# One core, two trunk branches: part of a modulation summed on VectorE, attention that rests at the end of gate sums, and position-bias transfers spread out

## The chip, the cores and the metric

One NeuronCore of a Trainium2 chip runs the whole program; seven other cores are idle. The metric is the time of one execution on the device, in microseconds (us), of which the median of several runs is taken. Smaller is better. All arithmetic is fp32: where TensorE multiplies, a number is split into a high part H and a low part L, and three products (H·H, L·H, H·L) stand for one.

## The reference, cut to what matters

One layer of a diffusion backbone is applied to 128 context tokens and 256 latent tokens, of width 2048. Each of the two token sets has its own condition vector.

```python
m = silu(cond) @ w_mod + b_mod            # 2048 x 12288: sh1, sc1, g1, sh2, sc2, g2
h = rms_norm(x, n1) * (1 + sc1) + sh1     # "norm 1"
q, k, v, u = split(h @ w_in)              # w_in 2048 x 4096
attn = neighbourhood or context attention, 16 heads of 64, with a position bias rpb
x = x + g1 * ((sigmoid(h @ w_gate) halves * (attn @ w_na, fft(u) @ w_fnet)) @ w_o)
h2 = rms_norm(x, n2) * (1 + sc2) + sh2
x = x + g2 * ((silu(g) * a) @ w_down),  a, g = split(h2 @ w_gate_up)
```

Norm 1's modulation needs sh1 and sc1, 2048 channels each, for both conditions. The channels are cut into 16 tiles of 128, called k-tiles here.

## The kernel before

The order of instructions on each engine is written out by hand, by Python generators. A **unit** is one load of weights, two k-tiles of 512 columns (one in places), as the tile `wraw`. `next_unit` is called before TensorE's products of each unit: ScalarE casts `wraw` into `wh`, VectorE subtracts into `wl` (both for a unit two ahead, `split_unit`), then work beside the products is ticked, and the next load is issued. `Paced` turns a generator into such work: at each tick `due` grows by `rate`, and once `due` is at least `least`, whole steps are run until less than one is left. The list `front` is ticked three times in a unit (twice in `next_unit`, once in `mid_unit`), the list `behind` once.

The input projection goes over k-tiles in four groups (`GROUPS`: 1, 2, 4 and 9 k-tiles), each of them over eight column chunks: 8, 8, 16 and 40 units. Products of a chunk gather in three PSUM buffers `mm` (of four), one for each 128 tokens; at the end of a chunk's group VectorE adds them to `acc` (L682).

`prep` (the generator `prepare`) makes norm 1's tokens beside that. For each entry of `MODS` (one k-tile, then five times three), `mod_sums` streams the columns of `w_mod` for sh1 and sc1 in (tile `wm`, four buffers) and lets TensorE multiply them with the condition vectors `csz`, into one PSUM tile (L404); ScalarE copies the sums out (`mrow`, L412), TensorE gathers them with a selector (L420, `sel`), three small VectorE operations make shift and scale, and `modulate` writes H and L of the k-tile's tokens. When `prep` ends, `rows` begins: it makes the other four modulations (sh2, sc2, g1, g2) on VectorE, a product and sum over `wmr` of 128 x 1024 at a time (`accr`, L327 and L329), and adds up over partitions with a matmul against ones (L338).

In the last group of the input projection `expand_rpb` copies the position bias in DRAM, seven transfers `s_rpb<-in_rpb` (L250), one in each unit. After it come the gates: eight blocks of eight units over `w_gate`, where `front` holds the Fourier branch and then attention (`br_work`) and `rows`. Each block fills all four `mm` buffers, and they are copied out in its last unit (`gst`, L1032), by ScalarE or, for the first two, by VectorE when attention has lately taken exponentials:

```python
(nc.vector.tensor_copy if f < 2 and any(soft) else nc.scalar.copy)(st, po[f][:, :TOK])
```

A pair of heads goes through attention in the ticks of the string `PAIR`: `s0 m0` are scores and maxima, `e0 i0` exponentials and inverses, `t0` the transposes, and so on. The rest of the program (projections, `w_o`, norm 2, SwiGLU) isn't touched.

Of the kernel before, what the change touches and what calls it, by code (L numbers as in the profile page):

```python
# [13 lines left out]
F32 = mybir.dt.float32  # L14
F32R = mybir.dt.float32r
AF = mybir.ActivationFunctionType
ALU = mybir.AluOpType
# [22 lines left out]
GROUPS = [(0, 1), (1, 2), (3, 4), (7, 9)]  # L40
ORDER = [6, 7, 0, 1, 2, 3, 4, 5]
DUE = [-1.4, 0, 0, 0]
PREP = [1.75, 1.8, 1.8, 1.8]
PAIR = "qk,b,pv,s0 m0,e0 i0,lq,s1 m1,e1 i1,,t0 lb,v,,t1,lv,"


# [55 lines left out]
def trunk_kernel(ctx: ExitStack, tc: tile.TileContext, io: dict):  # L102
# [163 lines left out]
    with ExitStack() as ph:  # L266
# [22 lines left out]


        ROWS = (2, 4, 3, 5)

        def row_weights():

# [77 lines left out]
        def depth_of(n):  # L372

            return 4 if n == 1 else 2

        def mod_weights(alloc):


            def load(kt0, n, k0):
                w, nk = n * P, depth_of(n)  # L380
                wm = alloc([P, 2, nk, w], "wm")
                for ty in range(2):
                    col = ty * D + kt0 * P
                    nc.sync.dma_start(
                        wm[:, ty],
                        w_mod[k0 * P : (k0 + nk) * P, col : col + w].rearrange("(k p) n -> p k n", p=P),
                    )
                return wm

            return Ahead(load, [(kt0, n, k0) for kt0, n in MODS for k0 in range(0, KT, depth_of(n))], 0)  # L390

        def mod_sums(src, kt0, n, alloc, out):

# [3 lines left out]
            for k0 in range(0, KT, nk):  # L397
                _, wm = src.take()
                for kk in range(0, nk, 2):
# [13 lines left out]
                        out.append(rows)  # L413
                    yield

        def mod_cols(kt0, n, rows):
# [12 lines left out]
            d = msc[0][:, kt0 : kt0 + n, :]  # L429
            nc.vector.tensor_add(d, m[:, :, 1], bc(bcol[:, KT + kt0 : KT + kt0 + n]))  # L430
            nc.vector.scalar_tensor_tensor(
                out=d, in0=d, scalar=1.0, in1=bc(ng[:, 0, kt0 : kt0 + n]), op0=ALU.add, op1=ALU.mult
            )
            yield


        with ExitStack() as pha:
            wmp = phm.enter_context(tc.tile_pool(name="wmp", bufs=4, side="right"))
            cpool = pha.enter_context(tc.tile_pool(name="cpool", bufs=12))
            tmp = pha.enter_context(tc.tile_pool(name="tmpa", bufs=2))  # L440

# [128 lines left out]
            def prepare():  # L570

                follow = columns_and_tokens(*MODS[0])
                while prepared[0] < 1:
                    yield next(follow)
                for k0, n in MODS[1:]:
                    for _ in mod_sums(src, k0, n, wme, sums):
                        next(follow, None)
                        yield
                    follow = columns_and_tokens(k0, n)
                    while k0 == 1 and prepared[0] < 3:  # L580
                        yield next(follow)
                for _ in follow:
                    yield

            prep = Paced(prepare())
            rows_psum["tile"] = md_tile

            def rows_and_columns():
# [63 lines left out]
            for gi, (k0, n) in enumerate(GROUPS):  # L652
                prep.due, prep.rate = DUE[gi], PREP[gi]
                prep.least = 3.6 if gi else 1
                if gi == len(GROUPS) - 1:
                    behind.append(Paced(expand_rpb()))
                    new_ring()
                for rate, ci in zip(CHUNKS, ORDER):
                    if gi == len(GROUPS) - 1:
# [153 lines left out]
                values()  # L813

        qks, vs, biases = [], [], []
        soft = deque(maxlen=3)

        def load_qk(hp):
# [27 lines left out]
        def attention_pair(hp, wk, values_before):  # L846
# [151 lines left out]
                    ("s", scores), ("m", maxima), ("e", exps), ("i", inverses), ("t", keys_first))},  # L998
            }
            for tick in PAIR.split(","):  # L1000
                for w in tick.split():
                    work[w]()
                soft.append("e" in tick)
                yield
# [13 lines left out]
        for fc8 in range(8):  # L1018
            po = [mm_tile() for _ in range(4)]
            sts = []  # L1020
            for u in range(0, KT, 2):
                wH, wL = next_unit()
                for f in range(4):
                    s = slice(f * P, (f + 1) * P)
                    if f == 2:
                        mid_unit()
                    for kk in range(2):
                        k = u + kk
                        mm3(po[f][:, :TOK], wH[:, kk, s], wL[:, kk, s], hH[k], hL[k], k == 0, k == KT - 1)
# [6 lines left out]
        br_work.drain()  # L1036
        front.clear()
        behind.append(rows)
        pha.close()
# [368 lines left out]
```

## Time and profile before

| | |
|---|---|
| median of 3 runs | 2051.44 us (2049.2 to 2052.01) |
| the profiled execution | 2052.19 us, of which the span of the trace 2050.4 |
| TensorE (PE) busy | 2025.8 us, 99% of the span |
| VectorE (DVE) busy | 1248.0 us, 61% |
| ScalarE (ACT) busy | 757.9 us, 37% |
| DMA read and written | 390.46 MB, mean 190 GB/s |

The profile is of one execution. A group row of it says how often an instruction of one line and shape ran, its busy time, its mean, and how long the engine had idled before it and for whom. A timeline row gives the start (from the span's begin), the duration, engine, line, what it writes and reads, and in brackets the idle time before it. Matmuls overlap in their pipeline, so a matmul's cost is read from the distance between starts and not from its duration. L404 means line 404 of the kernel before.

### The profile page before, as it was taken

The page shows a single profiled execution, that of the slowest core. Times are in us where ns is not written, and L with a number is a line of the kernel's source. Part 1 is how long each engine was busy: PE and PEld are TensorE (multiplying, and loading weights), DVE is VectorE, ACT ScalarE, POOL GpSimd, SP SyncE. Part 2 cuts the span into 40 slices and gives each one's busy share as a digit, 9 for nine tenths or more (in the row PEclk, how much of TensorE's full clock was granted, in tenths as well). Part 3 has the DMA queues.
Part 4 walks back from the last instruction along what each step waited for, and adds up shares of the span by engine and source line. Part 5 has one row for each costly group of instructions (what it writes and reads, how often), then busy time and mean ns, then how long its engine had stood idle before and what let it go on. Part 6 is the DMA issues. An engine that isn't in the chain of part 4 may idle for free.

```text
span 2050.4 us, 27528 instructions
## 1 busy us (share of the span) xinstructions
PE 2025.8 (99%) x10986; PEld 1843.8 (90%) x10986; DVE 1248.0 (61%) x1528; ACT 757.9 (37%) x1135; POOL 43.1 (2%) x92
## 2 busy tenths in 40 slices
PE   7999999999999999999999999999999999999999
PEld 4668788999999999889998999899989998999897
DVE  4746889788987777765854444545454334333456
ACT  4433232456665434334523332222222232223222
POOL 1000000000001000010000000000000000000000
PEclk9999999999999999999999999999999999999999
DMA  9996979677776776754455555455554444444453
GB/s 332 328 338 222 309 232 315 215 217 212 228 212 181 258 248 194 250 168 154 124 167 156 152 163 155 144 153 155 155 163 134 124 129 127 129 128 123 136 163 123
DMA packets 220384, 390.46 MB, mean 190 GB/s; under 512 B 28464, under 2 KB 77632, under 8 KB 220256
## 3 DMA queue, kind: packets, MB, share of 16 engines
q1 hardware_dynamic: 213088, 382.13, 59.5%
q10 hardware_dynamic: 4672, 6.31, 0.9%
q8 instruction: 86, 1.41, 0.3%
q0 software_dynamic: 2496, 0.27, 0.1%
q14 instruction: 42, 0.34, 0.1%
HBM read 371.81 MB, written 20.51 MB: 191 GB/s over the span
## 4 chain that ended last, share of the span: by engine, by line
PE 94%; DMA 3%; DVE 2%; ACT 1%; issue 0%; SPq 0%; ACTq 0%; DVEq 0%
PE mm L147 19%; PE mm L149 19%; PE mm L148 19%; PE at L147 11%; PE at L149 11%; PE at L148 11%; PE at L404 1%; DMA wm<-in_w_mod 1%; DMA wraw<-in_w_in 1%; PE at L893 1%; PE at L979 1%; PE at L958 1%; DMA wmr<-in_w_mod 1%; DVE accr L329 0%; DMA xc<-in_x_prompt 0%
## 5 line engine op out<-in xcount | busy, mean ns | idle before, releaser
L144 DVE TENSOR_TENSOR wl<-wraw,wh 128x1024 fp32r<-128x1024 f32 (+1 forms) x464 | 559.1, 1205 | 668.5 <-ACT wh L143 667.3
L143 ACT CAST wh<-wraw 128x1024 fp32r<-128x1024 f32 (+1 forms) x464 | 480.9, 1038 | 1032.0 <-PE at L148 272.9
L147 PE MATMUL mm<-hH,wh 128*128 128x384 f32 x1152 | 389.4, 338 | 2.4 <-DVE gst L1032 2.4
L149 PE MATMUL mm<-hH,wl 128*128 128x384 f32 x1152 | 385.5, 335 | 0.0
L148 PE MATMUL mm<-hL,wh 128*128 128x384 f32 x1152 | 385.2, 334 | 0.0
L329 DVE SCALAR_TENSOR_TENSOR accr<-wmr,csz,accr 128x1024 f32<-128x1024 f32 x240 | 304.8, 1278 | 5.2 <-DMA wmr<-in_w_mod 5.1
L147 PEld LDWEIGHTS mm<-hH,wh 128*128 128x128 f32 x1152 | 216.3, 188 | 8.1 <-issue 4.3
L148 PEld LDWEIGHTS mm<-hL,wh 128*128 128x128 f32 x1152 | 216.4, 188 | 0.0
L149 PEld LDWEIGHTS mm<-hH,wl 128*128 128x128 f32 x1152 | 216.2, 188 | 0.0
L147 PE MATMUL at<-hH,wh 128*128 128x384 f32 x640 | 213.9, 334 | 0.0
L149 PE MATMUL at<-hH,wl 128*128 128x384 f32 x640 | 213.9, 334 | 0.0
L148 PE MATMUL at<-hL,wh 128*128 128x384 f32 x640 | 213.8, 334 | 0.0
L147 PE MATMUL mm<-wh,hH 128*128 128x512 f32 x404 | 160.8, 398 | 1.9 <-ACT hH L548 1.2
L148 PE MATMUL mm<-wl,hH 128*128 128x512 f32 x404 | 158.1, 391 | 2.8 <-DVE wl L144 2.8
L149 PE MATMUL mm<-wh,hL 128*128 128x512 f32 x404 | 158.4, 392 | 0.7 <-DVE hL L144 0.4
L147 PE MATMUL mm<-wh,cH 128*128 128x512 f32 x352 | 137.1, 389 | 0.0
L149 PE MATMUL mm<-wh,cL 128*128 128x512 f32 x352 | 137.0, 389 | 0.0
L148 PE MATMUL mm<-wl,cH 128*128 128x512 f32 x352 | 137.0, 389 | 0.0
L147 PEld LDWEIGHTS at<-hH,wh 128*128 128x128 f32 x640 | 120.1, 188 | 1.0 <-ACT wh L143 0.8
L148 PEld LDWEIGHTS at<-hL,wh 128*128 128x128 f32 x640 | 120.1, 188 | 0.2
L149 PEld LDWEIGHTS at<-hH,wl 128*128 128x128 f32 x640 | 120.1, 188 | 0.0
L147 PEld LDWEIGHTS mm<-wh,hH 128*128 128x128 f32 x404 | 76.0, 188 | 25.6 <-issue 3.1
(283 smaller groups left out, 2633.5 us busy)
## 6 DMA issues: line engine op xcount, KB each, us to landing
wraw<-in_w_gate_up SPq DMA_DIRECT2D x176, 512.0 KB, 3.7
wmr<-in_w_mod SPq DMA_DIRECT2D x128, 512.0 KB, 4.9
wraw<-in_w_down SPq DMA_DIRECT2D x88, 512.0 KB, 3.7
wraw<-in_w_gate SPq DMA_DIRECT2D x64, 512.0 KB, 4.3
wm<-in_w_mod SPq DMA_DIRECT2D x80, 384.0 KB, 6.7
wraw<-in_w_in SPq DMA_DIRECT2D x56, 512.0 KB, 5.8
wraw<-in_w_o SPq DMA_DIRECT2D x32, 512.0 KB, 4.7
wraw<-in_w_fnet_proj SPq DMA_DIRECT2D x16, 512.0 KB, 4.9
```

What stands on the lines that cost most here:

```text
L143: nc.scalar.copy(H, x)
L144: nc.vector.tensor_sub(L, x, fr(H))
L147: nc.tensor.matmul(out, aH, bH, start=start, stop=False)
L148: nc.tensor.matmul(out, aH, bL, start=False, stop=False)
L149: nc.tensor.matmul(out, aL, bH, start=False, stop=stop)
L329: nc.vector.scalar_tensor_tensor(out=acc[:, cnd], in0=wm, scalar=sc, in1=acc[:, cnd], op0=ALU.mult, op1=ALU.add)
L404: nc.tensor.matmul(pm[q : q + 32, :w], csz[:, k, :], wm[:, ty, kk + par, :], start=k < 2, stop=k >= KT - 2, tile_position=(0, q), skip_gro ...
L893: nc.tensor.matmul(po[j][:, cols], qx[rows[j], q], kx[rows[j], k], start=i == 0, stop=i == 2, tile_position=(j * HD, 0),)
L958: nc.tensor.transpose(o[:, i * P : (i + 1) * P], sc[:, j, c0 : c0 + P], ident)
L979: nc.tensor.matmul(po[j][:, CTX:TOK].rearrange("p (t q) -> p t q", t=2), w[1 + kc], x.rearrange("p (t b) q -> p t b q", t=2)[:, :, 2 * kc ...
```

## The change

Three things are done.

1. The last entry of `MODS` (k-tiles 13 to 15) leaves `mod_sums`. A new generator `late_sums` loads its weights in 32 pieces `wd` of 128 x 384 (192 KB, five buffers; before: eight tiles `wm` in 16 transfers of 384 KB), and VectorE multiplies and sums them for both conditions into four accumulators `late`, which live in the buffers of tokens not yet made. It is ticked in `behind` from the second group on, 1.6 pieces in a unit. When all are summed, `late_rows` adds up over partitions with four matmuls against `hot` (a column of ones at the condition's place), ScalarE copies the sums out, and `mod_cols` goes on as before. `prep` goes at 1.6 instead of 1.8 steps in a unit in the third and fourth group.
2. In the last unit of each gate block, a tick of attention that takes exponentials waits three ticks, and `rows` runs only once three steps are due.
3. The seven `s_rpb` transfers go one in five units.

```diff
-PREP = [1.75, 1.8, 1.8, 1.8]
+PREP = [1.75, 1.8, 1.6, 1.6]
+LATE = 1.6
...
+        def late_sums(kt0, n):
...
+            got = Ahead(load, [(k, ty) for k in range(KT) for ty in range(2)], 5)
+            yield
+            for k in range(KT):
+                for ty in range(2):
+                    if k + ty:
+                        got.more()
+                    _, wd = got.take()
+                    for a, sc in zip(late_acc[ty], (csz[:, k, cnd : cnd + 1] for cnd in range(2))):
+                        if k == 0:
+                            nc.vector.tensor_scalar_mul(a, wd, sc)
+                        else:
+                            nc.vector.scalar_tensor_tensor(
+                                out=a, in0=wd, scalar=sc, in1=a, op0=ALU.mult, op1=ALU.add
+                            )
+                    yield
+        def late_rows(kt0, n, alloc, out):
...
+            for ty in range(2):
+                for cnd, a in enumerate(late_acc[ty]):
+                    q = 32 * (2 * ty + cnd)
+                    nc.tensor.matmul(
+                        pm[q : q + 32, :w], hot[:, cnd], a, start=True, stop=True,
...
+            rows = alloc([P, w], "mrow")
+            nc.scalar.copy(rows, pm[:, :w])
...
-                for k0, n in MODS[1:]:
+                for k0, n in MODS[1:-1]:
...
-                for _ in follow:
+                yield from follow
+                while late.live:
+                    late.step()
                     yield
+                late_rows(*MODS[-1], wme, sums)
+                yield
+                yield from columns_and_tokens(*MODS[-1])
...
+                if gi == 1:
+                    behind.append(late)
                 if gi == len(GROUPS) - 1:
-                    behind.append(Paced(expand_rpb()))
+                    behind.append(Paced(expand_rpb(), 0.2))
...
             for tick in PAIR.split(","):
+                for _ in range(3 if ending[0] and "e" in tick else 0):
+                    yield
...
+                ending[0] = u == KT - 2
+                rows.least = 3 if ending[0] else 1
                 wH, wL = next_unit()
```

On TensorE, the last sums of the modulation stood before as a block of `wm` products, and two units later the selector; here are the rows around the selector in the third group (`mm` gathers the projection, `at` another PSUM tile):

```order
L147 MATMUL mm_1487<-wh_1409,hH_205_972 128x512
L148 MATMUL mm_1487<-wl_1410,hH_205_972 128x512
L149 MATMUL mm_1487<-wh_1409,hL_206_973 128x512
L420 MATMUL at_1516<-sel,mrow_1460 128x4 x3
L147 MATMUL mm_1485<-wh_1433,hH_209_986 128x512
L148 MATMUL mm_1485<-wl_1434,hH_209_986 128x512
```

And in the change, one unit later in the program:

```order
L148 MATMUL mm_1559<-wh_1501,hH_231_1059 128x512
L149 MATMUL mm_1559<-wl_1502,hH_231_1059 128x512
L150 MATMUL mm_1559<-wh_1501,hL_232_1060 128x512
L459 MATMUL at_1626<-late_670,hot 32x384
L459 MATMUL at_1626<-late_671,hot 32x384
L459 MATMUL at_1626<-late_672,hot 32x384
L459 MATMUL at_1626<-late_673,hot 32x384
L471 MATMUL at_1633<-sel,mrow_1631 128x4 x3
L148 MATMUL mm_1619<-wh_1560,hH_162_723 128x512
```

The selector now follows the matmuls whose copied sums it reads at once. The 64 products of `wm` for the last entry are gone from the rows between; from the second group to this place the blocks of such small products between the units number eight, where they were ten.

On VectorE, in the second group of the input projection, two chunks followed each other like this (`wl` the low weights of a unit to come, `xT` the scaling of a token tile, `acc` the sums of a chunk):

```order
L144 TENSOR_TENSOR wl_750<-wraw_604,wh_749 128x1024
L527 TENSOR_TENSOR xT_267<-xT_267,rB_310 128x384
L682 TENSOR_TENSOR acc_455<-acc_455,mm_746 128x512
L682 TENSOR_TENSOR acc_455<-acc_455,mm_747 128x512
L682 TENSOR_TENSOR acc_455<-acc_455,mm_748 128x512
L144 TENSOR_TENSOR wl_781<-wraw_641,wh_780 128x1024
```

and in the change, at the chunk before that one and this one:

```order
L445 TENSOR_SCALAR late_670<-wd_674,csz 128x384
L445 TENSOR_SCALAR late_671<-wd_674,csz 128x384
L445 TENSOR_SCALAR late_672<-wd_676,csz 128x384
L445 TENSOR_SCALAR late_673<-wd_676,csz 128x384
L742 TENSOR_TENSOR acc_424<-acc_424,mm_707 128x512
L742 TENSOR_TENSOR acc_424<-acc_424,mm_708 128x512
L742 TENSOR_TENSOR acc_424<-acc_424,mm_709 128x512
L145 TENSOR_TENSOR wl_777<-wraw_611,wh_776 128x1024
L579 TENSOR_TENSOR xT_274<-xT_274,rB_317 128x384
L447 SCALAR_TENSOR_TENSOR late_670<-wd_678,csz,late_670 128x384
L447 SCALAR_TENSOR_TENSOR late_671<-wd_678,csz,late_671 128x384
L742 TENSOR_TENSOR acc_462<-acc_462,mm_773 128x512
```

Two or four operations on `late` stand in each unit ahead of the sums that empty PSUM.

On ScalarE, at the end of the fourth gate block, exponentials (`sc,sm<-sc,mx`) and their scaling stood ahead of the copies `gst`:

```order
L143 CAST wh_4599<-wraw_4347 128x1024
L932 ACTIVATE sc_4438,sm_4603<-sc_4438,mx_4597 128x384 x2
L942 ACTIVATE sc_4438<-sc_4438,sm_4603 128x384 x2
L1032 COPY gst_4636<-mm_4116 128x384
L1032 COPY gst_4644<-mm_4117 128x384
```

In the change they come behind the next unit's cast:

```order
L144 CAST wh_4683<-wraw_4434 128x1024
L1097 COPY gst_4711<-mm_4197 128x384
L1097 COPY gst_4719<-mm_4198 128x384
L1100 DMA s_gate_94<-gst_4695 128x384
L1100 DMA s_gate_94<-gst_4703 128x384
L1100 DMA s_gate_94<-gst_4711 128x384
L1100 DMA s_gate_94<-gst_4719 128x384
L144 CAST wh_4733<-wraw_4480 128x1024
L993 ACTIVATE sc_4506,sm_4737<-sc_4506,mx_4681 128x384 x2
L1003 ACTIVATE sc_4506<-sc_4506,sm_4737 128x384 x2
```

Attention's later steps move with them. There are two such rests in the program, and attention ends two units later than before, with two and a half units of gate products still behind it.

## Rows read from the trace of the kernel before

**Rows 1.** The page: the span, the engines' busy times, and the shares of the chain of work that ended last.

```profile
span 2050.4 us, 27528 instructions
PE 2025.8 (99%) x10986; PEld 1843.8 (90%) x10986; DVE 1248.0 (61%) x1528; ACT 757.9 (37%) x1135; POOL 43.1 (2%) x92
...
PE 94%; DMA 3%; DVE 2%; ACT 1%; issue 0%; SPq 0%; ACTq 0%; DVEq 0%
```

**Rows 2.** All waits of TensorE from 165 to 2040 us: who waited for whom, us in total, times, the longest.

```profile
PE mm L148 <- DVE wl L144: 2.8, 2, 2.0
PE mm L147 <- DVE gst L1032: 2.4, 2, 1.5
PE at L149 <- DVE uL L144: 0.8, 1, 0.8
```

**Rows 3.** The timeline of TensorE around the last block of `wm` products but for the selector.

```profile
149.59 0.39 PE L148 MATMUL mm<-wl,hH 128*128 128x512 f32 x1
149.81 0.39 PE L149 MATMUL mm<-wh,hL 128*128 128x512 f32 x1
150.13 2.79 PE L404 MATMUL at<-wm,csz 128*32 128x384 f32 x32
152.85 0.50 PE L147 MATMUL mm<-wh,hH 128*128 128x512 f32 x1
153.19 0.40 PE L148 MATMUL mm<-wl,hH 128*128 128x512 f32 x1
```

**Rows 4.** Groups by shape, whole run: the sums over partitions that `rows` makes on TensorE.

```profile
L338 PE MATMUL at<-accr,ones 128*32 128x512 f32 x64 | 9.1, 605 | 0.0
```

**Rows 5.** The timeline of TensorE at two selectors: one right behind the products whose sums it reads, one two units behind them.

```profile
46.06 1.25 PE L404 MATMUL at<-wm,csz 128*32 128x384 f32 x8
47.90 0.83 PE L420 MATMUL at<-sel,mrow 128*128 128x4 f32 x6 [0.58 <-ACT mrow L412]
...
161.14 0.73 PE L420 MATMUL at<-sel,mrow 128*128 128x4 f32 x6
```

**Rows 6.** Busy time of the engines in stretches: us, then PE, PEld, DVE, ACT and POOL busy, the granted clock, the DMA share, GB/s.

```profile
20.00:50.00 30.00, 26.65 (x153) 13.99 (x152) 13.96 (x27) 11.88 (x22) 0.00 (x0) 0.89 1.06 369
60.00:100.00 40.00, 39.92 (x245) 27.11 (x244) 27.23 (x42) 13.34 (x20) 0.00 (x0) 1.00 0.95 322
100.00:160.00 60.00, 60.00 (x354) 41.98 (x353) 29.09 (x42) 21.55 (x32) 0.00 (x0) 1.00 0.90 312
195.00:225.00 30.00, 30.00 (x134) 24.86 (x133) 23.60 (x22) 7.74 (x8) 0.00 (x0) 1.00 1.04 365
```

**Rows 7.** Groups by shape of VectorE, the first two from 60 to 100 us, the others of the whole run.

```profile
L144 DVE TENSOR_TENSOR wl<-wraw,wh 128x1024 fp32r<-128x1024 f32 x8 | 9.8, 1224 | 3.1 <-ACT wh L143 3.1
L527 DVE TENSOR_TENSOR xT<-xT,rB 128x384 f32<-128x384 f32 x5 | 2.8, 552 | 0.0
...
L329 DVE SCALAR_TENSOR_TENSOR accr<-wmr,csz,accr 128x1024 f32<-128x1024 f32 x240 | 304.8, 1278 | 5.2 <-DMA wmr<-in_w_mod 5.1
...
L327 DVE TENSOR_SCALAR accr<-wmr,csz 128x1024 f32<-128x1024 f32 x16 | 11.8, 746 | 0.0
```

**Rows 8.** First the timeline of SyncE, which issues the loads; then the chain of waits between 74 and 97 us (start, us, what); then DMA issues of the whole run with size and median time to landing.

```profile
72.28 4.57 SPq L384 DMA_DIRECT2D wm<-in_w_mod  x8
...
76.39 7.09 DMA wm<-in_w_mod
...
94.07 2.72 PE at L404 x32
...
wm<-in_w_mod SPq DMA_DIRECT2D x80, 384.0 KB, 6.7
...
wraw<-in_w_in SPq DMA_DIRECT2D x16, 256.0 KB, 6.5
```

**Rows 9.** Timelines around the longest wait of the middle of the run: SyncE's issues (two of the seven `s_rpb`), ScalarE's cast, VectorE, TensorE.

```profile
204.03 0.66 SPq L250 DMA_DIRECT2D s_rpb<-in_rpb  x1
...
208.09 0.55 SPq L250 DMA_DIRECT2D s_rpb<-in_rpb  x1
...
222.83 1.05 ACT L143 CAST wh<-wraw 128x1024 fp32r<-128x1024 f32 x1 [4.61 <-DMA wraw<-in_w_in]
...
224.12 2.48 DVE L329 SCALAR_TENSOR_TENSOR accr<-wmr,csz,accr 128x1024 f32<-128x1024 f32 x2 [3.89 <-DMA wmr<-in_w_mod]
...
228.31 1.22 DVE L144 TENSOR_TENSOR wl<-wraw,wh 128x1024 fp32r<-128x1024 f32 x1
...
229.58 0.50 PE L148 MATMUL mm<-wl,hH 128*128 128x512 f32 x1 [2.02 <-DVE wl L144]
```

**Rows 10.** Timelines at the ends of two gate blocks: ScalarE, VectorE and TensorE at 504 us, TensorE at 639 us.

```profile
503.87 1.12 ACT L942 ACTIVATE sc<-sc,sm 128x384 f32<-128x384 f32 x2 [0.23 <-DVE sm L940]
...
503.75 1.27 DVE L329 SCALAR_TENSOR_TENSOR accr<-wmr,csz,accr 128x1024 f32<-128x1024 f32 x1
504.94 1.02 DVE L1032 COPY gst<-mm 128x384 f32<-128x384 f32 x2
...
505.54 0.44 PE L147 MATMUL mm<-hH,wh 128*128 128x384 f32 x1 [1.48 <-DVE gst L1032]
...
639.42 0.44 PE L147 MATMUL mm<-hH,wh 128*128 128x384 f32 x1 [0.94 <-DVE gst L1032]
```

More of the change, by code (lines that the diff above doesn't have):

```diff
@@ L291, in trunk_kernel @@
         ROWS = (2, 4, 3, 5)
+        late_acc = []
+        hot = consts.tile([P, 2, 32], F32, tag="hot", name="hot")
+        nc.vector.memset(hot, 0.0)
+        for cnd in range(2):
+            nc.vector.memset(hot[:, cnd, cnd : cnd + 1], 1.0)
         def row_weights():
@@ L388, in load @@
                 return wm
-            return Ahead(load, [(kt0, n, k0) for kt0, n in MODS for k0 in range(0, KT, depth_of(n))], 0)
+            return Ahead(load, [(kt0, n, k0) for kt0, n in MODS[:-1] for k0 in range(0, KT, depth_of(n))], 0)
         def mod_sums(src, kt0, n, alloc, out):
@@ L414, in mod_sums, with load @@
                     yield
+        def late_sums(kt0, n):
+            w = n * P
+            def load(k, ty):
+                wd = wdp.tile([P, w], F32, tag="wd", name=nm("wd"))
+                c0 = ty * D + kt0 * P
+                nc.sync.dma_start(wd, w_mod[k * P : (k + 1) * P, c0 : c0 + w])
+                return wd
+            for ty in range(2):
+                late_acc.append(
+                    [hpool.tile([P, w], F32, tag=f"t{c}{KT - 3 + ty}", name=nm("late")) for c in "HL"]
+                )
[12 more added lines that the diff above has]
+                                out=a, in0=wd, scalar=sc, in1=a, op0=ALU.mult, op1=ALU.add
+                            )
+                    yield
+        def late_rows(kt0, n, alloc, out):
+            w = n * P
+            pm = at_tile()
+            for ty in range(2):
+                for cnd, a in enumerate(late_acc[ty]):
+                    q = 32 * (2 * ty + cnd)
+                    nc.tensor.matmul(
+                        pm[q : q + 32, :w], hot[:, cnd], a, start=True, stop=True,
+                        tile_position=(0, q), skip_group_check=True,
+                    )
+            rows = alloc([P, w], "mrow")
+            nc.scalar.copy(rows, pm[:, :w])
+            out.append(rows)
         def mod_cols(kt0, n, rows):
@@ L438, in trunk_kernel @@
             wmp = phm.enter_context(tc.tile_pool(name="wmp", bufs=4, side="right"))
+            wdp = phm.enter_context(tc.tile_pool(name="wdp", bufs=5, side="right"))
             cpool = pha.enter_context(tc.tile_pool(name="cpool", bufs=12))
@@ L581, in prepare @@
                         yield next(follow)
-                for _ in follow:
+                yield from follow
+                while late.live:
+                    late.step()
                     yield
+                late_rows(*MODS[-1], wme, sums)
+                yield
+                yield from columns_and_tokens(*MODS[-1])
             prep = Paced(prepare())
+            late = Paced(late_sums(*MODS[-1]), LATE)
             rows_psum["tile"] = md_tile
@@ L815, in trunk_kernel @@
         qks, vs, biases = [], [], []
+        ending = [False]
         soft = deque(maxlen=3)
@@ L1036, in trunk_kernel @@
         br_work.drain()
+        rows.least = 1
         front.clear()
```

## Prediction

> **What bounds the kernel now.** I read the page first: TensorE is busy for 2025.8 of 2050.4 us, and the chain of work that ended last lies on it for 94% [rows 1]. The reader is to see from this that time can be won only by taking work from TensorE or by closing its gaps. The list of its waits then says how much there is of the second kind: between 165 and 2040 us six waits, 2.8 us for low weights `wl`, 2.4 us for gate copies, 0.8 us for a Fourier operand [rows 2]. So no single edit can bring much there, and the work taken away has to be priced by the distance of starts. Last I read the stretch where work is added to other engines: from 60 to 100 us VectorE is busy for 27.2 of 40 us, from 100 to 160 for 29.1 of 60, and the DMA engines have shares of 0.95 and 0.90, where 1.06 with 369 GB/s is the most that a stretch shows [rows 6]. TensorE hardly waits there, yet both others have little left in the first 40 us. Whether they carry the new work is the question of this change.
>
> **The modulation's last entry.** 64 products of `wm` go. A block of 32 stands from 150.13 to 152.85 us, 2.72 us or 85 ns each [rows 3]; two such blocks are 5.4 us, all on TensorE's path. Entering a block costs 0.32 where a start otherwise follows after 0.22 to 0.23, leaving it 0.34 [rows 3], some 0.2 us for a block; the order shows two fewer, so another 0.4 us goes. Added are four matmuls against `hot`. In fp32 the trace shows two passes for one, so eight; by the rows of `rows`' sums, which are 512 wide, they cost at most 8 x 9.1 / 64 = 1.1 us [rows 4], by 85 ns each 0.7. I take 0.8. New too is a wait: the selector now comes right behind the matmuls whose sums ScalarE has first to copy. The nearest row has a gap of 0.58 us there, and the one that stands two units off has none [rows 5]. In the change a cast of 1.05 us [rows 9] is queued on ScalarE just ahead of that copy, so the bounds are 0.6 and 1.6; I take 0.9. Behind the waiting selector all of TensorE's queue stands still. Sum of this part: -5.4 - 0.4 + 0.8 + 0.9 = -4.1 us.
>
> **What VectorE gets for it.** 64 operations of 128 x 384, of which the trace has none. From above, the 1024-wide sum takes 1.28 us [rows 7]; that it were no faster at 384 bounds it. From below 0.28, the 1024-wide plain product (0.75) scaled by width. The nearest row by width is 0.55 (`xT`, two SBUF operands, 384), and I take that. About 22 fall between 60 and 100 us: 27.2 + 22 x 0.55 = 39.3 of 40 us, full to the brim; the other 42 find 29.1 + 23 of 60. What is queued behind a late operation on VectorE are the three `acc` sums, which free PSUM, and the next `wl`. Both have room: `wl` is made two units ahead (a unit is 18 products at 0.23, 4.1 us), and with four buffers for three tiles a unit's sums are wanted only well into the unit after. So I cost it at nothing; if the cover goes, each unit pays its excess.
>
> **What the DMA queue gets.** The bytes are the same, but come earlier: about 15 pieces of 192 KB, 2.9 MB, before 100 us, where those of the old entry all came later. 322 GB/s becomes 322 + 2.9 MB / 40 us = 395, above the 369 of the fullest stretch: 1.0 MB too much, 2.8 us. The cushion: the loads issued from 72.28 us on feed products at about 84 and at 94 us, their landing takes 6.7 us in the median, and the chain of waits has one of them landing at 83.5 [rows 8], where TensorE is about to want it. Of the 2.8 us I expect 0.5 to reach TensorE, between the bounds 0 and 2.8; later the groups stand a unit further apart, and 6.3 MB less is wanted. SyncE's queue also waits for the slot of a `wd` piece ahead of `wraw` and `wm`; the five buffers are about three units, so I cost that at nothing beyond it.
>
> *A rule against this.* The rows show 256 KB transfers landing after 6.5 us where 384 KB take 6.7 [rows 8], in a queue that is seldom empty [rows 6], so small pieces don't pay for themselves alone. The Trainium skill ("DMA: Bandwidth & Descriptors", section Bandwidth) wants transfers of 1 MiB or more, and gives 138 GB/s for 64 KB and 341 for 1 MB. By it the new pieces would move at perhaps two thirds of the rate (an estimate from that page); the trace doesn't show it at these sizes, and it is a rival below.
>
> **Gate ends.** At 505.54 and 639.42 us TensorE waits 1.48 and 0.94 us for VectorE's copies of the block's sums [rows 10]. At the first, scaling of exponentials (until 505) and an `accr` of 1.27 us stand ahead of the copies on ScalarE and VectorE. The change puts both behind the copies; the order shows it. Next late there is the copy itself, 0.5 us, under the products of the other tiles. I take -2.2 of the 2.4; bounds -2.4 and 0, the latter if other steps of attention now meet a block's end. The two units by which attention ends later are covered: two and a half units of products remain.
>
> **The bias transfers.** From 195 to 225 us the DMA share is 1.04 [rows 6], with transfers of `s_rpb` unit by unit. A `wraw` comes late, ScalarE's cast idles 4.61 us for it, a `wmr` stops VectorE for 3.89, and the `wl` behind them ends at 229.5, which costs TensorE 2.02 us [rows 9]. With one in five units this pile-up doesn't form: I take -2.0, bounds -2.0 and 0. The other wait for `wl` (0.8 us) and the Fourier one stay. `rows` starts about two units later and moves as a whole; its results are wanted far behind.
>
> Sum: -4.1 + 0.5 - 2.2 - 2.0 = -7.8 us. Against the profiled 2052.19 that is 2044.4; that execution lies 0.75 above the median of the runs, so the prediction for the median is 2043.6 us.
>
> **Rivals.**
> *The loads bound the stretch up to 100 us.* For it: the DMA share of 0.95 there; against it: transfers issued 10 us ahead. The whole 2.8 us shows instead of 0.5, and the selector waits 1.6 instead of 0.9: -4.8, or 2046.6.
> *Small transfers are slow (the rule).* If a 192 KB piece took the queue as long as a 384 KB one, 1.07 us at 369 GB/s instead of 0.53, 15 pieces would add 8 us to the 2.8. Less some 3 us of cushion, about 7.8 arrive: the gain is gone, 2051. Against it are the landing times [rows 8].
> *The two later gaps only move.* Attention and `rows` stand otherwise against the blocks, and a full queue can form at another place; four of the 4.2 us come back: 2047.6. For it: VectorE is busy 23.6 of 30 us there [rows 6].
> *VectorE becomes the bound, and the kernel slower.* Its place is the second group of the input projection, 60 to 100 us, where it decides from 0.55 us for an operation on: above that, 22 operations no longer fit into 40 us, the `acc` sums come late and PSUM stops TensorE. At the upper bound of 1.28 us it is 22 x 0.73 = 16 us: -8 + 16, or 2059.5. At 0.9 it would just eat the gain. Against it: two rows of 1024 and 384 give 1.05 ns a column, so 0.6 at most.
>
> **Chances.** Forecast 0.60 (own range 2041 to 2046.5), the loads 0.15, the rule 0.04, the gaps that move 0.13, VectorE 0.08. Less than 0.2%, 4.1 us, is about what a measurement of this kernel can't tell from no change: faster than that is below 2047.3. Nearly all of the forecast and of the loads, and a little under half of the gaps that move, are that: 0.58 + 0.13 + 0.05 = 0.76; the same for the rest and the rule, 0.16; VectorE is the slower side, 0.08. The range runs from 2040.5, where every bound falls well, a third wait of 0.8 us goes too and the runs lie as far down as the lowest of before (2.2 us under the median), to 2049.5, which takes in the loads and the gaps that move.
>
> **What will show it.** Group rows: the products of `wm` 256 instead of 320, the late sums at 0.5 to 0.6 us each. In the timeline of TensorE: no wait over 1 us between 60 and 165 us but for one of about 0.9 at the selector behind `late`. From 60 to 100 us VectorE at 38 to 40 of 40 us. In the list of waits after 165 us: `gst` gone or under 0.3 us, one `wl` of 0.8 left. TensorE's busy time down by about 4.5 us. I'm wrong if `wm` or `acc` ends waits of TensorE up to 165 us that add up to 3 us or more, if `gst` or `wl` stand in the list with 2 us at other places, or if the late sums take 0.8 us.

## The result: slower, and the profile after

The changed kernel takes 2059.82 us in the median of four runs (2058.91 to 2063.64), the kernel before beside it 2051.73; the ratio is 1.0046, with a 95% interval of 1.0034 to 1.0059. I had forecast 2043.6, faster, in a range up to 2049.5. The profiled execution took 2058.91 us. It is the fastest of the four, so that its trace explains 6.7 us (spans of 2057.1 and 2050.4) and not the whole 8.1 between the medians. In what follows "the changed kernel" is this one, and lines of its code are its own (L404 of before is L410, L338 is L344, L682 is L742, L1032 is L1097).

First the page of the changed kernel: the span, the engines, the chain that ended last.

```profile
span 2057.1 us, 27536 instructions
PE 2025.6 (98%) x10930; PEld 1846.1 (90%) x10930; DVE 1280.2 (62%) x1595; ACT 756.5 (37%) x1135; POOL 44.1 (2%) x92
...
PE 91%; DMA 3%; DVE 3%; ACT 1%; issue 1%; SPq 1%; ACTq 0%; DVEq 0%
```

Beside [rows 1] the reader sees that TensorE is as busy as ever (2025.8 before), though 64 products went, and that the span is 6.7 us longer. Busy time can only stay while work goes if what is left ran slower. Then all waits of TensorE from 60 to 2040 us (who for whom, us in total, times, the longest), which answer to [rows 2]:

```profile
PE mm L148 <- DVE gst L1097: 4.0, 2, 3.6
PE mm L148 <- DVE acc L742: 3.3, 1, 3.3
PE at L344 <- DVE accr L335: 2.1, 1, 2.1
PE at L150 <- DVE uL L145: 0.8, 1, 0.8
PE mm L149 <- DVE wl L145: 0.8, 1, 0.8
PE at L471 <- ACT mrow L418: 0.6, 1, 0.6
PE at L471 <- ACT mrow L464: 0.6, 1, 0.6
PE at L344 <- DVE pt L145: 0.5, 1, 0.5
PE at L410 <- DMA wm<-in_w_mod: 0.2, 1, 0.2
```

The wait of 2.0 us for `wl` has gone, as forecast. Three new ones stand there, each for VectorE: `acc`, `gst` and `accr`. Where the time went stage by stage is read from the start of the same weight split `wl` (the k-th of 464, counted from 0) in both traces:

| k-th `wl` | start before | after | difference | what lies between |
|---|---|---|---|---|
| 8 | 52.04 | 50.97 | -1.1 | start of the run; differs between executions by as much |
| 36 | 191.31 | 193.18 | +1.9 | modulation with late sums: +2.9 |
| 60 | 284.84 | 283.95 | -0.9 | bias transfers: -2.8, of which 2.0 are the wait |
| 88 | 405.99 | 404.98 | -1.0 | |
| 144 | 702.34 | 705.85 | +3.5 | gate blocks with attention: +4.5 |
| 172 | 823.39 | 830.02 | +6.6 | gates' products, where `rows` sums: +3.1 |

From there to the end the difference stays at 6.6. So four places make the result: the bias transfers, which gain, and three stops of TensorE, which are shown now.

**The stop for `acc` at 153 us.** Timelines of the changed kernel, VectorE first (start, us, engine, line, out<-in, how many in a row), then TensorE:

```profile
148.86 1.22 DVE L145 TENSOR_TENSOR wl<-wraw,wh 128x1024 fp32r<-128x1024 f32 x1 [0.74 <-ACT wh L144]
150.29 0.56 DVE L145 TENSOR_TENSOR hL<-hf,hH 128x384 fp32r<-128x384 f32 x1 [0.21 <-ACT hH L144]
151.72 0.56 DVE L145 TENSOR_TENSOR hL<-hf,hH 128x384 fp32r<-128x384 f32 x1 [0.87 <-ACT hH L144]
153.16 0.56 DVE L145 TENSOR_TENSOR hL<-hf,hH 128x384 fp32r<-128x384 f32 x1 [0.88 <-ACT hH L144]
153.63 2.20 DVE L447 SCALAR_TENSOR_TENSOR late<-wd,csz,late 128x384 f32<-128x384 f32 x4
155.75 1.88 DVE L742 TENSOR_TENSOR acc<-acc,mm 128x512 f32<-128x512 f32 x3
...
152.79 0.39 PE L150 MATMUL mm<-wh,hL 128*128 128x512 f32 x1
156.49 0.50 PE L148 MATMUL mm<-wh,hH 128*128 128x512 f32 x1 [3.31 <-DVE acc L742]
157.41 0.63 PE L148 MATMUL mm<-wh,hH 128*128 128x512 f32 x1
157.83 0.63 PE L149 MATMUL mm<-wl,hH 128*128 128x512 f32 x1
```

`prep` prepares three tokens in one unit here. Their three `hL` stand in VectorE's queue, and each waits for ScalarE, so that 1.7 us of work last from 150.3 to 153.7. Behind them come four late sums, 2.2 us, and only then the three `acc` sums, which empty the PSUM buffers that TensorE needs at 153.0. It stands for 3.31 us.

The same unit of the kernel before (its `wl` is the one with k = 27, as here) holds one token, and the `acc` sums wait for TensorE:

```profile
151.32 1.23 DVE L144 TENSOR_TENSOR wl<-wraw,wh 128x1024 fp32r<-128x1024 f32 x1 [2.84 <-ACT wh L143]
152.75 0.56 DVE L144 TENSOR_TENSOR hL<-hf,hH 128x384 fp32r<-128x384 f32 x1 [0.21 <-ACT hH L143]
154.54 0.69 DVE L682 TENSOR_TENSOR acc<-acc,mm 128x512 f32<-128x512 f32 x1 [1.23 <-PE mm L149]
```

So the change puts two more tokens into this unit, and not only the late sums. Before, three tokens stood in one unit too, at 95 us, right ahead of `acc` sums; there a block of 32 `wm` products stood on TensorE beside them (94.00 to 96.72 us), and no wait shows. The three tokens at 150 us in the changed kernel have no such block beside them. That this cover is what is missing wasn't tried by itself.

After the stop, TensorE's starts are 0.43 us apart instead of 0.23, and the windows show why (from:to, us, busy times of PE, PEld, DVE, ACT and POOL, the granted clock, the DMA share, GB/s):

```profile
153.00:156.00 3.00, 0.17 (x1) 0.00 (x0) 2.84 (x6) 1.07 (x2) 0.00 (x0) 1.00 0.07 10
157.00:158.00 1.00, 1.00 (x4) 0.77 (x4) 1.00 (x3) 0.00 (x0) 0.00 (x0) 0.56 0.99 373
158.00:160.00 2.00, 2.00 (x7) 1.54 (x6) 2.00 (x4) 0.00 (x0) 0.00 (x0) 0.50 0.32 56
161.00:162.00 1.00, 1.00 (x6) 0.84 (x5) 0.00 (x0) 0.87 (x1) 0.00 (x0) 1.00 0.77 295
```

TensorE idled from 153 to 156, and from 157 the granted clock is at 0.50, the lower of its two levels (1.2 GHz), until shortly after 160. Eight starts lose 0.2 us each: 1.6 us on top of the 3.3. This is the busy time that hides in the page.

**The end of a gate block at 590 us.** VectorE and TensorE of the changed kernel:

```profile
588.47 1.26 DVE L335 SCALAR_TENSOR_TENSOR accr<-wmr,csz,accr 128x1024 f32<-128x1024 f32 x1
589.64 0.87 DVE L966 SCALAR_TENSOR_TENSOR sc<-at,rq,bp 128x256 f32<-128x256 f32 x2
590.94 0.95 DVE L981 TENSOR_REDUCE mx<-sc 128x2 f32<-128x768 f32 x1 [0.43 <-ACT sc L971]
591.87 1.23 DVE L145 TENSOR_TENSOR wl<-wraw,wh 128x1024 fp32r<-128x1024 f32 x1
593.02 1.02 DVE L1097 COPY gst<-mm 128x384 f32<-128x384 f32 x2
...
593.71 0.41 PE L148 MATMUL mm<-hH,wh 128*128 128x384 f32 x1 [3.56 <-DVE gst L1097]
594.54 0.52 PE L148 MATMUL mm<-hH,wh 128*128 128x384 f32 x1
594.86 0.52 PE L149 MATMUL mm<-hL,wh 128*128 128x384 f32 x1
```

Exponentials (`e0`) were taken in the unit before, so the copies of the first two tiles go to VectorE; but the tick that meets the block's last unit is `s1 m1`, scores and maxima, which the rest doesn't hold back. They and a weight split stand ahead of the copies. Again some ten starts follow at 0.32 instead of 0.17 us: 3.6 + 1.6. The ends of [rows 10] are better: 1.48 became 0.46, and 0.94 went. With 0.5 us for `pt` ahead of other sums of `rows`, at 485 us, this comes to some 3.7 of the 4.5 us in the table; the rest I can't place.

**The sums of `rows` at 759 us.** TensorE of the changed kernel, then VectorE's last `accr`, then the same matmuls in the kernel before:

```profile
758.91 1.05 PE L344 MATMUL at<-accr,ones 128*32 128x512 f32 x4
762.07 1.05 PE L344 MATMUL at<-accr,ones 128*32 128x512 f32 x4 [2.10 <-DVE accr L335]
760.73 1.28 DVE L335 SCALAR_TENSOR_TENSOR accr<-wmr,csz,accr 128x1024 f32<-128x1024 f32 x1
```

```profile
751.24 1.06 PE L338 MATMUL at<-accr,ones 128*32 128x512 f32 x8
```

Before, these matmuls were issued two units behind the last `accr`; after, one unit (counted in the code as it is built). VectorE isn't done, TensorE waits 2.1 us in the middle, and the eight matmuls, which otherwise run side by side in 1.06 us, take that time twice.

### The profile page after: what moved, and what is told of

Read it like the earlier page. It is cut to its first block, busy times and chain, and to the rows that moved or that the text cites. A ratio compares the mean times of both kernels' runs of the same rounds, so it can differ in the third digit from the quotient of the medians.

```text
span 2057.1 us, 27536 instructions
## 1 busy us (share of the span) xinstructions
PE 2025.6 (98%) x10930; PEld 1846.1 (90%) x10930; DVE 1280.2 (62%) x1595; ACT 756.5 (37%) x1135; POOL 44.1 (2%) x92
## 4 chain that ended last, share of the span: by engine, by line
PE 91%; DMA 3%; DVE 3%; ACT 1%; issue 1%; SPq 1%; ACTq 0%; DVEq 0%
PE mm L148 18%; PE mm L150 18%; PE mm L149 18%; PE at L148 11%; PE at L150 11%; PE at L149 11%; DMA wm<-in_w_mod 2%; PE at L410 1%; DMA wd<-in_w_mod 1%; DVE accr L335 1%; DVE wl L145 1%; PE at L1019 0%; PE at L954 0%; PE at L344 0%; DMA s_gate<-gst 0%
```

## Experiments

All ran as the two kernels did, beside the kernel before on the same chip; a ratio is to it. "Span" is that of the profiled execution. My theory by now: three separate collisions in VectorE's in-order queue, none of them a lack of VectorE time on average, plus one gain of 2 us.

**The parts alone.** `late` is the kernel before with the late sums and PREP, LATE; `rest` with `ending` and `rows.least`; `rpb` with this line; `norest` is the changed kernel without `ending` and `rows.least`.

```diff
-                    behind.append(Paced(expand_rpb()))
+                    behind.append(Paced(expand_rpb(), 0.2))
```

> The kernel before with the late sums alone (VectorE's sums, PREP and LATE; no rest at gate ends, the bias transfers as before). Theory, read from the changed kernel's trace: 64 products and their blocks go (-5.8 us), the matmuls against hot and the selector's wait come (+1.9), and one stop of TensorE near 153 us comes, 3.3 us of waiting for acc and some 1.6 us of products at the lower clock after it (+4.9): +1.0 us. Since the rows stage starts some 6 us later with this part, I also expect here the split of two groups of rows sums that the changed kernel shows at 759 us (+3.1): +4.1 in all. Rival, the loads are what costs: waits for wm and wd in the first 165 us of over 2 us and no stop for acc, and the rows sums undisturbed: +1 or less with another wait list. Second rival, the rows split belongs to the rest at gate ends: +1.0 here.

> The kernel before with the rest at gate ends alone (ending and rows.least). Theory: the waits at the two ends of before (1.5 and 0.9 us) go, and the later steps of attention meet another end, where VectorE copies the sums behind scores, maxima and a weight split: the changed kernel shows 3.6 us there and 1.6 us of slow products: +4.4 in its gate stage. Alone, with attention at the same phase, I expect +3 to +5 us and the gst wait at about 590 us. Rival, the new wait at 590 us comes from the rows stage standing elsewhere, not from attention's phase: then this kernel has no gst wait over 0.5 us, and -2.2 us.

> The kernel before with the bias transfers one in five units alone. Theory: the wait of 2.0 us for wl at 227 us goes and nothing else changes: -2.0 us. Rival, the queue is full there anyway, and another piece comes late: a wait for wl or accr of 1 us or more between 195 and 345 us, and 0 to -1 us.

> The changed kernel without the rest at gate ends (late sums and bias transfers only). Theory, if the split of the rows sums at about 755 us belongs to the later start of the rows stage: +1.0 - 2.0 + 3.1 = +2 us against the kernel before, and the gst waits of before (1.5 and 0.9) are back, perhaps at other places. Rival, it belongs to the rest: -1.0 us, the sums of rows in one piece.

Measured: `late` 1.0013 (1.0004 to 1.0022), `rest` 1.0014 (1.0006 to 1.0023), `rpb` 0.9989 (0.9980 to 0.9997), `norest` 1.0011 (1.0003 to 1.0020). The waits fall where the theory puts them: `late` and `norest` both show 3.3 us for `acc` and 2.1 for `accr`, `rest` neither, but 3.0 for `gst` at 590 us. So the split of the sums belongs to the later start of `rows`, which `late` brings, and the wait at 590 to the rest. The bias transfers are worth what was forecast. The sizes are less clean. For `late`, 4.1 us were expected; its ratio gives 2.7, its medians 4.5, and the interval (0.8 to 4.5) holds both. Its trace shows two gains that I hadn't counted: no stall at 227 us either, and waits of 0.7 and 0.1 us at the gate ends instead of 1.5 and 0.9. By their ratios `late`, `rest` and `rpb` come to 3.3 us in sum, the changed kernel to 9.4: the parts share gains (227 us, gate ends) that the whole has only once.

**What stands ahead of `acc`.** `first` is `norest` with the late sums ticked ahead of `prep`, `half` is `norest` with half of them (it leaves out the second condition's from the second k-tile on).

```diff
-                    behind.append(late)
+                    behind.insert(0, late)
```

```diff
-                    for a, sc in zip(late_acc[ty], (csz[:, k, cnd : cnd + 1] for cnd in range(2))):
+                    for a, sc in zip(late_acc[ty][: 1 + (k == 0)], (csz[:, k, cnd : cnd + 1] for cnd in range(2))):
```

> Late sums and bias transfers (no rest), with the late sums queued on VectorE ahead of the step that prepares tokens instead of behind it. Theory, VectorE's order makes the stop near 153 us: 1.7 us of hL subtractions, stretched to over 4 us by waiting for ScalarE, and then 2.2 us of late sums stand ahead of the acc sums. Put first, the late sums fall into the time in which hL waits, and the acc sums come some 2.2 us earlier: the 3.3 us become 1 or less, the lower clock after it shrinks or goes, and the time falls by 2 to 4 us against the same kernel with the other order. Rival, VectorE has too much work or a late weight piece holds it: the stop keeps its 3.3 us, wherever the sums stand.

> Late sums and bias transfers (no rest); the late sums of the second condition are left out from the second k-tile on, so that VectorE has 34 operations instead of 64 for the same loads. Three theories of the stop near 153 us. Order (what stands ahead of the acc sums in that one unit): 1.1 us fewer stand there, so 3.3 becomes about 2.2. Load (VectorE has more work than time in that stretch): the stop goes to 0.3 or less. Transfers (a late piece of the weights): 3.3 stays. Each tenth of it also shows in the time, with up to 1.6 us of lower clock behind it.

The wait of TensorE in `half`:

```profile
PE mm L148 <- DVE acc L742: 2.3, 1, 2.3
```

That is the 2.2 of the order theory, not the 0.3 of a full VectorE nor the 3.3 of a late transfer: what counts is what stands ahead of `acc` in this one unit. The time of `half` is 1.0002 (0.9993 to 1.0010), where `norest` has 1.0011. The late sums follow each other at 0.53 us; without any of the four, 1.2 of the 3.3 us would be left (an estimate from these two numbers), and that would be the part of the two more tokens. `first` was a miss: also 2.3 us instead of 1 or less, and no faster, 1.0021 (1.0012 to 1.0030). Its trace shows that `prep` itself steps a late sum behind its tokens (155.94 us, two operations) once no `mod_sums` are left; I had overlooked these two lines of `prepare`. And it shows a loss that I had overlooked as well, since the list of waits has only 0.4 us of it: from their first start to the next start behind them, three blocks of 32 `wm` products take 4.0, 4.1 and 3.3 us, where [rows 3] has 2.72. That is 3.2 us for weights that come late.

**Phase or rows at the gate ends.** `shift` is the kernel before with three empty ticks ahead of attention, and no rest; `rest1` has the rest without `rows.least`.

```diff
                 values = None
+                for _ in range(3):
+                    yield
                 for hp in range(8):
```

> The kernel before with attention started three steps later, and no rest anywhere. Theory, the wait for gst at 590 us is a matter of attention's phase against the blocks: the shift alone brings it, 2.5 to 3.5 us at about 590 us and the lower clock behind it, and the ends at 505 and 639 us wait less than in the kernel before (under 1 us together): +2.5 to +5 us, as with the rest alone. Rival, the steps of the rows stage held back at block ends (rows.least) make it: then no gst wait over 1 us at 590, and -1 to -2 us.

> The kernel before with the rest of attention at gate ends, but with the rows stage stepping as ever (no rows.least). Theory of the phase: the gst wait at 590 us stays at 2 us or more, since scores, maxima and the weight split stand ahead of the copies without any accr too; the time within 1.5 us of the kernel with both. Rival, accr held back makes it: no wait over 1 us there, and 3 us less than with both.

`shift` 1.0027 (1.0016 to 1.0038), `rest1` 1.0025 (1.0015 to 1.0035). TensorE's waits in `shift`, then the one of its products at 594 us:

```profile
PE mm L147 <- DVE gst L1034: 4.7, 2, 3.1
PE mm L147 <- ACT gst L1034: 1.6, 1, 1.6
...
594.04 0.69 PE L147 MATMUL mm<-hH,wh 128*128 128x384 f32 x1 [3.09 <-DVE gst L1034]
```

Without any rest, three ticks of shift bring the wait at 590 us, so attention's phase decides; the ends at 455 and 502 us were worse than I expected (1.6 each). In `rest1` the wait at 590 is 4.0 us and one at 502 us is 2.1, where `rest` has 3.0 and 0.9: holding `rows` back made them shorter, not longer. By the ratios `rest1` is 2.3 us slower than `rest`, more than the 1.5 that I had allowed, but the intervals overlap. A rest of three ticks at one end is a shift of three ticks for all later ends.

**The distance of the sums.** `gap` adds an empty step behind the last `accr`, `r115` changes a rate, both on `norest`.

```diff
                 yield
+                yield
                 o = rows_psum["tile"]()
```

```diff
-RATES = [1.5, 0.5, 1.1, 0.937, 0.452]
+RATES = [1.5, 0.5, 1.15, 0.937, 0.452]
```

> Late sums and bias transfers (no rest), with one more empty step between the last accr sum and the matmuls that add it up. Theory, the stop at 755 us comes from two steps of the rows stage in one unit, which put these matmuls a unit after the accr instead of two, while VectorE runs a unit behind: with the third step the wait for accr goes and the eight matmuls run side by side again, -3.1 us against the kernel without that step. Rival, VectorE is late there for another reason (the sums of gates): a wait of 1 us or more stays.

> Late sums and bias transfers (no rest) with the rows stage at 1.15 instead of 1.1 steps a unit in the gates' products: the sums at about 753 us then stand two units behind the last accr instead of one. Theory: the 2.1 us of waiting go and the eight matmuls run in one piece again, 3.1 us less than without this edit, about the time of the kernel before; the stop near 153 us stays at 3.3. Rival, as with the extra step, another place comes late: a new wait of 1 us or more behind 700 us.

In both the wait for `accr` is gone and the sums run in one piece. `r115`: 1.0001 (0.9993 to 1.0010), span 2048.6 against the 2051.4 of `norest`. `gap`: 1.0007 (0.9998 to 1.0016), but `rows` ends later by its added steps, and a transpose of its columns now waits 2.3 us at 941 us for a row that has only just gone through DRAM. The 3.1 us expected of `gap` didn't come, and neither did the rival written for it, a wait that stays at this place. A new wait elsewhere is the rival of `r115`, which was written when `gap` had been seen, and there none came.

**Can the late sums pay?** `rowsrpb` has no late sums and no rest: the kernel before with `rpb`, the rate 1.15, and `rows` a unit later, `Paced(rows_and_columns(), RATES[0], 1)`. This puts `rows` just where `r115` has it. `spread` is `r115` with the late sums behind `acc` and the tokens in two units:

```diff
-                if gi == 1:
-                    behind.append(late)
...
+                        if gi:
+                            late.tick()
...
+                prep.least = 1
                 yield from follow
+                prep.least = 3.6
```

> The kernel before with the bias transfers one in five units and the rows stage starting one unit later (at 1.15 steps a unit in the gates' products, so that its sums keep two units), without late sums and without rest. Theory: the waits at the gate ends depend on where accr and weight splits stand on VectorE; at this place of the rows stage the late-sum kernels show 0.7 and 0.1 us instead of 1.5 and 0.9. So -2.0 for the bias transfers and -1.6 for the gate ends: -3.6 us. Rival, the two ends are shorter there because attention stands otherwise: 2.4 us of gst waits as before, and -2.0 us.

> Late sums and bias transfers (no rest), with three edits: the late sums step behind the acc sums of the unit instead of ahead of them, the last three tokens before them are prepared in two units instead of in one, and the rows stage steps at 1.15 instead of 1.1 a unit in the gates' products, which puts its sums two units behind the last accr as in the kernel before. Order theory: the acc sums near 153 us are late by less than 0.3 us, no lower clock there, and the rows sums run in one piece: 3.3 + 1.6 + 3.1 = 8 us less than the same kernel without the edits, which is 5 to 7 us under the kernel before. Load theory: VectorE is full, and the time comes back as waits for wl or acc of 2 us or more between 100 and 185 us; then only the 3.1 of the rows come.

`rowsrpb` takes 2047.27 us against 2050.76, 0.9982 (0.9974 to 0.9991), as expected. It beats both kernels. Its waits of TensorE from 60 to 2040 us are these four and no others:

```profile
PE at L149 <- DVE uL L144: 0.8, 1, 0.8
PE mm L148 <- DVE wl L144: 0.8, 1, 0.8
PE mm L147 <- DVE gst L1032: 0.7, 1, 0.7
PE at L338 <- DVE pt L144: 0.3, 1, 0.3
```

`spread` takes 2050.39, 0.9998 (0.9989 to 1.0006): not the 5 to 7 us less that the order theory gave. The wait for `acc` did shrink to 0.5, but the first lines of its list are

```profile
PE at L459 <- DVE late L447: 2.0, 1, 2.0
PE at L410 <- DMA wm<-in_w_mod: 0.9, 4, 0.3
```

The sums moved back are now themselves late for their matmuls. Here the load theory has its share: from 155 to 168 us VectorE is busy without a break. The larger loss is behind the 0.9 us for `wm`. That list counts the time in which TensorE's matmuls idle; the loads of their weights (PEld) waited longer, here from 60 to 165 us:

```profile
PEld at L410 <- DMA wm<-in_w_mod: 5.0, 8, 0.9
```

By starts, the blocks of 32 `wm` products at 70, 95 and 123 us take 4.6, 3.3 and 4.7 us instead of 2.72, 4.5 us more in all; in `rowsrpb` every such block takes 2.72. The last run gives the matmuls against `hot` a unit more, and prepares the last tokens one in a unit:

```diff
+                prep.least = 1
+                for _ in range(3):
+                    yield
                 late_rows(*MODS[-1], wme, sums)
...
-CHUNKS = [1.8, 1.8, 1.8, 1.4, 1.4, 0.95, 0.95, 1.6]
+CHUNKS = [1.8, 1.8, 1.8, 1.8, 1.7, 1.1, 1.1, 1.6]
```

> As the kernel with three edits (late sums behind acc, tokens in two units, rows at 1.15), and further the matmuls against hot one unit later, tokens 13 to 15 one a unit behind them, and the first rates of the rows stage raised so that its sums keep their place among the gates. Theory: the late sums pay once nothing waits for them. From the traces up to the first rows sums: 64 products and two entries go (22.3 - 18.1 and 0.6 us), the matmuls cost 1.0, the two selector waits 1.2, waits for modulation weights up to 0.9: -0.6 to -1.6 us against the kernel with the rows and the bias transfers alone, and 2 to 4 us less than with the three edits. Rival: what the late sums take from VectorE and the queue comes back whatever stands behind them, as waits for late, acc, wl or wm of 2 us or more in all before 185 us: then it stays 2 us or more above the kernel with the rows and the bias transfers alone.

`calm` takes 2054.98, 1.0021 (1.0012 to 1.0030), but not because of the late sums. Its longest waits:

```profile
PE at L344 <- DVE accr L335: 3.9, 1, 3.9
PE mm L148 <- DVE gst L1097: 1.4, 1, 1.4
```

`rows` starts three units later than in `rowsrpb`, and with the rates that I raised to make up for it VectorE is late at the first sums of `rows`, at 260 us. Up to there (the `wl` with k = 48) `calm` is 0.4 us behind `rowsrpb`, where it had begun 0.6 us later: with both stops gone, the late sums are about even, neither the gain of the theory nor the 2 us of its rival. But the rival's cause is there: the blocks of 32 `wm` products take 4.2, 3.4 and 3.4 us, 2.9 us more than in `rowsrpb`, of which the list shows 0.4. What the late sums save on TensorE, late weights take back. Whether some arrangement of all this ends below `rowsrpb` was not found.

## Why the prediction was wrong, step by step

*The products of `wm`: right.* By starts, as the prediction counts them, the blocks of `wm` products from 60 to 165 us took 22.3 us and now take 18.2. Two of the blocks that are left have grown by 1.1 us in all (see the DMA queue), so 5.3 us went, of 5.4 forecast. The matmuls against `hot` took 1.3 instead of 0.8. The selector behind them waited 0.57 instead of 0.9, but the selector of the entry before, which I hadn't counted, now also follows its own products directly and waits 0.60 (0.5 more). With 0.4 for the two entries, as forecast, this part without its stop is -5.3 - 0.4 + 1.3 + 0.6 + 0.5 = -3.3, not -4.1.

*"What VectorE gets for it ... I cost it at nothing": the step that failed.* The price of a late sum was near enough, as this group of the changed kernel shows, and so was VectorE's load from 60 to 100 us, 35.8 of 40 us where I had 39.3 (the window behind it, columns as before):

```profile
L447 DVE SCALAR_TENSOR_TENSOR late<-wd,csz,late 128x384 f32<-128x384 f32 x60 | 33.3, 612 | 0.7 <-DMA wd<-in_w_mod 0.7
```

```profile
60.00:100.00 40.00, 39.91 (x244) 27.36 (x237) 35.81 (x62) 13.28 (x20) 0.00 (x0) 1.00 1.06 376
```

I named what stands behind a late sum, the `acc` sums, and answered with averages: so many operations in so many microseconds. I did not read the worst unit, the one in which three tokens are prepared, though the order of instructions shows it and the trace of before has such units, with `hL` waiting for ScalarE. There 4.9 us pass between the start of a `wl` and the end of the tokens' `hL`, and the fourth PSUM buffer doesn't cover 2.2 us more. Nor did I ask beside which units the tokens would stand once the last entry's `wm` blocks were gone. Cost: 3.3 us and 1.6 of slow clock. `half` shows that the late sums' place ahead of `acc` makes part of it, some two thirds by the estimate above; `spread`, which moves both the late sums and the tokens, leaves 0.5 us. With the -3.3 and the 1.1 of `wm` below this makes +2.7 of the +2.9 in the table.

*The DMA queue: right in kind, twice as dear.* From 60 to 100 us the share is 1.06 at 376 GB/s, as full as the fullest stretch of before. The list of waits has 0.2 us for `wm` (0.5 forecast), but the starts show more:

```profile
120.30 2.77 PE L410 MATMUL at<-wm,csz 128*32 128x384 f32 x28
123.26 0.84 PE L410 MATMUL at<-wm,csz 128*32 128x384 f32 x4 [0.18 <-DMA wm<-in_w_mod]
124.03 0.50 PE L148 MATMUL mm<-wh,hH 128*128 128x512 f32 x1
```

A block of 32 takes 2.72 us in [rows 3]. This one takes 3.7, as its last weights come late, and one at 93 us 2.9: 1.1 us in all, between the bounds of 0 and 2.8. I had also cost at nothing what the slots of `wd` do to SyncE's queue; from 55 to 165 us it stood there for 26.8 us, up to 6.2 at a time, until a late sum had freed one. Whether this makes `wm` late wasn't tried. The rival of slow small pieces fell: with the 192 KB pieces the queue moves more than the 369 GB/s of its fullest stretch before.

*"Gate ends ... I take -2.2": the second step that failed.* The two ends lost 1.0 and 0.9 us as forecast, but I took the rest for something local. It moves every later step of attention by three ticks, and the next collision, 3.6 us and its slow clock, was twice the two that went. My rival of gaps that only move had this mechanism, with 4 us coming back; from -2.2 to the +4.5 of the table it is 6.7. The bound of 0 was too kind: a moved collision can be longer than the one removed.

*"`rows` ... moves as a whole": the third.* It started one unit later, as a whole, but its rate of 1.1 steps a unit puts two steps into about every tenth unit, and the later start put such a unit between the last `accr` and its sums. A distance of two units became one: 3.1 us.

*The bias transfers: right.* 2.0 forecast; `rpb` measured a ratio of 0.9989, 2.3 us (0.6 to 4.1). But on top of the late sums nothing clear is left of it (`late` 1.0013, `norest` 1.0011): in `late` the stall at 227 us doesn't form.

*The rivals.* The slower side, "VectorE becomes the bound", came out within 0.4 us of the time, 2059.5, for another reason: not the second group, not a dear operation. I had given it 0.08. Of what I listed as proof of error, two came true: `acc` with over 3 us ahead of 165 us, and `gst` with over 2 us at another place. The prediction's "six waits" behind 165 us are five [rows 2]; no term hangs on it.

## What to carry to other kernels

Where work is added to an in-order queue of an engine that is not full on average (62% here), look for the one unit in which most stands ahead of what the bounding engine waits for, and add up durations and waits there; the average over the stage doesn't show it. Work that is taken from the bounding engine may also be work behind which another engine hid, as the units at 95 and 153 us suggest. A pause in work that runs beside other work is a shift of all that follows, so its other meetings have to be read again too, and a fractional rate hides distances that a shift changes. Late weights are read from the distance of starts: of 4.5 us that they cost `spread`, the list of idle times shows 0.9. The best of 13 trials took no work from TensorE at all: it moved two side jobs apart.

## What was not expected of the hardware

A stop costs more than its length. Behind the wait of 3.3 us at 153 and of 3.6 at 590 us the granted clock was 0.50 for some three microseconds; behind the 2.0 us at 227 us in the kernel before and the 2.1 at 759 in the changed one it stayed at 1.00, while `half` shows 0.50 behind 2.3 us, and `half` and `first` behind the same 2.1 us for `accr`, at 757 us. In `first` it stayed at 1.00 behind the 2.3 us for `acc`. So the length of a wait alone doesn't decide it here. In `rest`, whose profiled execution was 2.5 us above its median, it stayed low for almost seven (592 to 599 us). The kernels that stop spread more: 2052.1 to 2057.9 us for `late`, 2046.5 to 2048.3 for `rowsrpb`. In `late` the six executions with a mean clock of 0.995 or 0.996 took 2056.1 us on average, the five with 0.997 or 0.998 2053.6, so the clock is part of this spread.

Matmuls with 32 columns of weights, put on four places of the array, run side by side: eight in 1.06 us, and four in 1.05. With a wait in their middle the eight took 2.1 us.
